# A float32 encoder layer on one core: the x tiles load first, and the Strassen operand T2 of both FFNs is formed tile by tile

## The chip, the cores and the metric

The kernel runs on one core of one Trainium2 chip. The metric is the device time of one execution in microseconds (us); the median of three runs before the change is 1804.01 us (1801.94 to 1806.21). A core has five engines that work through their own instruction lists in order: TensorE (PE, matmuls and transposes), VectorE (DVE), ScalarE (ACT), GpSimd (POOL) and SyncE (SP, which here only issues DMAs). They wait for one another through semaphores.

## The reference

One layer on x of 1024 tokens by 1024 channels, all float32:

```python
x = x + 0.5 * swiglu(rmsnorm(x, ffn1_norm), ffn1_w_gate, ffn1_w_up, ffn1_w_down)   # hidden 2816
h = rmsnorm(x, mix_norm) @ w_in             # -> u, v, c_q, c_kv, k_rope
y_a = gmlp_mixer(u, v, ...)                 # gated MLP over blocks of 128 tokens
y_b = mla_mixer(c_q, c_kv, k_rope, ...)     # 8 heads, block-causal attention
x = x + concat(rmsnorm(y_a), rmsnorm(y_b)) @ w_out
x = x + 0.5 * swiglu(rmsnorm(x, ffn2_norm), ffn2_w_gate, ffn2_w_up, ffn2_w_down)
x = rmsnorm(x, final_norm)
```

with `swiglu(h, g, u, d) = (silu(h @ g) * (h @ u)) @ d`.

## The kernel before

**Numbers.** A float32 operand is split into a high and a low part (`h` and `l`); every product is three 128x512 matmuls, high by high, high by low and low by high. The split is one ACT cast (the high part) and one DVE subtraction (the low part).

**Gate and up.** `GateUp` ("a" is FFN1, "b" is FFN2) computes the gate and up projections in the seven-product scheme of Strassen. The transposed, normalised x is cut into four blocks: B11 and B21 are the two channel halves of tokens 0 to 511 (tiles 0 to 3, 128 tokens each), B12 and B22 those of tokens 512 to 1023 (tiles 4 to 7). The x operands are B11, B21, B22 and the sums T3 = B22 - B12, T2 = T3 + B11, T1 = B12 - B11, T4 = B21 - T2. The weight columns are worked through in 11 units u of 256 gate and 256 up columns; each unit has the products P1 (B11), P2 (B21), P6 (T2), P5 (T1), P7 (T3), P3 (B22) and P4 (T4), 24 matmuls each. `GU_ORDER` begins with P1 and P2 of u0 and of u1 (`EARLY`), which need tiles 0 to 3 only, and then takes P6, P5, P7, P3, P4 of u0, the same of u1, and so on. So the 96 matmuls of `EARLY` stand between the arrival of tiles 0 to 3 and the first use of T2.

**The x operands.** `XOps.tile(i)` normalises one tile (a Square with a sum on ACT, a mean on DVE, the reciprocal root on POOL, `xn` on DVE), transposes it in eight PE transposes and copies it into two blocks on ACT. After tile 3 it splits B11 and B21. `XOps.sums()`, called in the second step of FFN1 and FFN2 after tile 7, forms all sums and splits from whole blocks, in halves of 128x1024: about 20 DVE operations and 10 ACT casts.

**Where tiles come from.** In FFN1 they are loads of x (`xa0` to `xa7`) in one SP queue with the weights (`raw`, four DMAs of 512 KB per unit). A unit's weights are loaded nine steps ahead (`LEAD_LOAD`), its sums three and its splits two steps ahead. In FFN2 tile t comes out of `out_tile(t)`: 48 matmuls of the out-projection (`wo`), an addition of the residual, which is loaded from `x1d` (`x2_t`), a store to `x2d`, and then `xo2.tile(t)`.

**What sets the order.** The code is a list of `Step`s. A tile framework then reorders the instructions of each engine by its own estimate and assigns buffers and semaphores, so that the instruction order differs from the order of the code. SP issues its DMAs in order, and a DMA whose buffer is not free holds all that follow it.

## Time and profile before

| | |
|---|---|
| median of 3 runs | 1804.01 us (1801.94 to 1806.21) |
| the profiled execution | 1804.58 us |
| its span | 1802.8 us |
| PE busy | 1731.7 us, 96% |
| DVE busy | 1122.5 us, 62% |
| ACT busy | 750.3 us, 42% |
| POOL busy | 124.9 us, 7% |

A busy time is the sum over the instructions of an engine. [...] A timeline row gives the start, the duration, the engine, the line, the operation with output and input, and in brackets the idle time of the engine just before and who ended it.

### The profile page before, as it was taken

To read this page: it belongs to the slowest core of one execution; us is meant where nothing else is said; L and a number is where in the kernel's file an instruction comes from. 1 tells how busy PE (TensorE), PEld (TensorE's weight loads), DVE (VectorE), ACT (ScalarE), POOL (GpSimd) and SP (SyncE) were. 2 spreads that over 40 slices of the span, in tenths; PEclk is the share of its full clock that TensorE was granted. 3 is DMA by queue.
4 is the path that set the end of the run, shared out by engine and by line. 5 is a ranking of instruction groups with operands and counts; after the bars stand their busy time and mean duration, and the time that the engine had idled before them with its cause. 6 is when DMAs were issued, how large, how long until landed. Compare 5 with 4: busy or idle time off the path is not lost.

```text
span 1802.8 us, 21101 instructions
## 1 busy us (share of the span) xinstructions
PE 1731.7 (96%) x8196; PEld 1444.9 (80%) x8196; DVE 1122.5 (62%) x1481; ACT 750.3 (42%) x1139; POOL 124.9 (7%) x242
## 2 busy tenths in 40 slices
PE   6799999999999999997999999889999999999988
PEld 5688888888888888896888888668888888888876
DVE  6875466654687667458676544665556655658753
ACT  6533233334343353355666733433233333433442
POOL 2000000000000004225000500000000000000000
PEclk9899999999999999998999899989999999999999
DMA  6132423225834520300000452131323222783431
GB/s 204 59 117 88 135 93 117 88 94 210 292 129 158 192 88 20 109 13 1 1 1 7 142 174 71 53 118 58 134 101 111 88 95 87 245 308 102 158 121 47
DMA packets 123493, 199.51 MB, mean 111 GB/s; under 512 B 11008, under 2 KB 57600, under 8 KB 123392
## 3 DMA queue, kind: packets, MB, share of 16 engines
q1 hardware_dynamic: 122816, 197.11, 32.0%
q8 instruction: 64, 1.05, 0.2%
q10 hardware_dynamic: 576, 1.05, 0.2%
q14 instruction: 37, 0.30, 0.1%
HBM read 143.07 MB, written 55.05 MB: 110 GB/s over the span
## 4 chain that ended last, share of the span: by engine, by line
PE 91%; DVE 4%; ACT 2%; DMA 1%; SPq 1%; issue 1%; POOL 1%; POOLq 0%; ACTq 0%; DVEq 0%
PE psum L438 45%; PE psum L569 8%; PE psum L570 8%; PE psum L567 7%; PE psum L693 2%; PE psum L691 2%; PE psum L692 2%; PE psum L1093 2%; PE psum L1091 2%; PE psum L1090 2%; PE psum L993 2%; PE psum L963 1%; PE psum L286 1%; PE psum L1002 1%; PE psum L1003 1%; PE psum L965 1%
## 5 line engine op out<-in xcount | busy, mean ns | idle before, releaser
L454 DVE TENSOR_TENSOR P_b<-psum,P_b 128x1024 f32<-128x1024 f32 x33 | 40.3, 1222 | 62.8 <-PE psum L438 62.7
L454 DVE TENSOR_TENSOR P_a<-psum,P_a 128x1024 f32<-128x1024 f32 x33 | 40.3, 1221 | 55.6 <-PE psum L438 55.5
L968 DVE TENSOR_REDUCE nm<-psum 128x1 f32<-128x128 f32 (+3 forms) x64 | 47.8, 753 | 27.9 <-PE psum L966 19.8
L444 ACT COPY P_a<-psum 128x1024 f32<-128x1024 f32 x33 | 33.5, 1014 | 68.6 <-PE psum L438 68.6
L444 ACT COPY P_b<-psum 128x1024 f32<-128x1024 f32 x33 | 33.5, 1014 | 68.1 <-PE psum L438 68.1
L455 ACT ACTIVATE P_a<-P_a 128x512 f32<-128x512 f32 x33 | 20.9, 634 | 96.8 <-DVE P_a L454 96.5
L455 ACT ACTIVATE P_b<-P_b 128x512 f32<-128x512 f32 x33 | 20.9, 633 | 96.4 <-DVE P_b L454 96.3
L277 DVE TENSOR_TENSOR pl<-psum,ph 128x384 fp32r<-128x384 f32 (+1 forms) x80 | 48.8, 629 | 11.6 <-ACT ph L276 11.3
L970 ACT ACTIVATE p<-psum,nm 128x128 f32<-128x128 f32 (+3 forms) x64 | 47.9, 749 | 18.9 <-DVE nm L968 17.1
L963 PE MATMUL psum<-kh,qh 96*128 96x512 f32 (+2 forms) x96 | 41.4, 431 | 11.8 <-ACT qh L951 8.1
L257 POOL TENSOR_TENSOR r_fin<-ms_fin,mhalf 128x1 f32<-128x1 f32 x8 | 6.0, 754 | 643.6 <-DVE ms_fin L255 643.6
L1090 PE MATMUL psum<-woh,yh 128*128 128x512 f32 x128 | 50.5, 397 | 0.0
L1091 PE MATMUL psum<-wol,yh 128*128 128x512 f32 x128 | 50.1, 393 | 0.0
L276 ACT CAST ph<-psum 128x384 fp32r<-128x384 f32 (+1 forms) x80 | 41.6, 550 | 9.0 <-PE psum L993 7.9
L438 PE MATMUL psum<-xT2h_f,S2h_b 128*128 128x512 f32 x88 | 35.4, 402 | 10.1 <-ACT S2h_b L423 10.1
L993 PE MATMUL psum<-ident,p 128*128 128x128 f32 x288 | 43.5, 280 | 1.4 <-ACT p L970 1.2
L1002 PE MATMUL psum<-ph,vv 128*128 128x256 f32 x160 | 44.7, 305 | 0.1
L1003 PE MATMUL psum<-pl,vv 128*128 128x256 f32 x160 | 43.5, 301 | 0.3 <-DVE pl L277 0.3
L257 POOL TENSOR_TENSOR r_m<-ms_m,mhalf 128x1 f32<-128x1 f32 x8 | 5.6, 704 | 551.3 <-DVE ms_m L255 551.3
L1093 PE MATMUL psum<-woh,yl 128*128 128x512 f32 x128 | 43.5, 395 | 0.0
L438 PE MATMUL psum<-xT2l_f,S2h_a 128*128 128x512 f32 x88 | 35.1, 399 | 8.3 <-DVE xT2l_f L361 8.3
L438 PE MATMUL psum<-xT1l_f,S1h_b 128*128 128x512 f32 x88 | 34.7, 396 | 6.0 <-DVE xT1l_f L361 6.0
(519 smaller groups left out, 5717.8 us busy)
## 6 DMA issues: line engine op xcount, KB each, us to landing
raw_a<-in_ffn_w_gate SPq DMA_DIRECT2D x22, 512.0 KB, 4.2
...
```

What stands on the lines that cost most here:

```text
L438: mm(o, lhs[:, 4 * m + k, :], rhs[:, k, :], start=pn in FIRST and n == 0, stop=n == 11, skip_group_check=True)
L444: nc.scalar.copy(ev[u, pn], bk)
L454: nc.vector.tensor_tensor(c, bk, c, op=ALU.add)
L567: mm(banks[t], hh[:, j, tl], dh[:, j, :], start=pn in DOWN_FIRST and c == 0 and j == 0, stop=False, skip_group_check=True)
L569: mm(banks[t], hh[:, j, tl], dl[:, j, :], start=False, stop=False, skip_group_check=True)
L570: mm(banks[t], hl[:, j, tl], dh[:, j, :], start=False, stop=c == 5, skip_group_check=True)
L993: nc.tensor.transpose(ps[:, i * P:(i + 1) * P], prs[j][:, c * P:(c + 1) * P], ident)
L1002: mm(acc[:, 0:256], mx["vv"][c][:, h, :], hi, start=i == 0, stop=False)
L1003: mm(acc[:, 0:256], mx["vv"][c][:, h, :], lo, start=False, stop=i == len(pts) - 1)
L1090: mm(pe[e], yh[:, k, :], wh[:, es], start=k == 0, stop=False)
L1091: mm(pe[e], yh[:, k, :], wl[:, es], start=False, stop=False)
L1093: mm(pe[e], yl[:, k, :], wh[:, e * 512:(e + 1) * 512], start=False, stop=k == KD - 1)
```

## The change

It does four things. First, in FFN1 the loads of `xa1`, `xa2` and `xa3` stand in a row ahead of the first unit's weights. Second, `XOps.tile` calls `second(i)` for the tiles 4 to 7, which forms T3, T2 with its split, and B21 - T2 for the 128 columns of that tile: four DVE operations and one ACT cast of 128x512 elements each. Third, `sums` is gone; T1, T3, B22 and T4 are made by `rest`, in the steps +2, +3, +3 and +4 of the FFN, and tied behind the last T2 operations by an issue order (`after`). Fourth, the weights of FFN2's first two units are loaded in the steps of out tile 6 and of P1(u0) rather than nine steps ahead of their products.

```diff
             if i == 3:
                 self.split("B11", self.b[0, 0])
                 self.split("B21", self.b[1, 0])
+            if i >= 4:
+                self.second(i, slice(c, c + P))
+
+        def second(self, i, cs):
+
+            b11, b12, b21, b22 = (v[:, :, cs] for v in (self.b[0, 0], self.b[0, 1], self.b[1, 0], self.b[1, 1]))
+            if i == 4:
+                self.t3 = tile_([P, 4, 512], f"t3_{self.nm}")
+                self.ops["T2"] = [tile_([P, 4, 512], f"xT2{n}_{self.nm}", F32R) for n in "hl"]
+            t3, hi, lo = (v[:, :, cs] for v in (self.t3, *self.ops["T2"]))
+            t2 = tile_([P, 4, P], f"t2{i}_{self.nm}")
+            nc.vector.tensor_tensor(t3, b22, b12, op=ALU.subtract)
+            nc.vector.tensor_tensor(t2, t3, b11, op=ALU.add)
+            self.last = (nc.scalar.copy(hi, t2), nc.vector.tensor_tensor(lo, t2, f(hi), op=ALU.subtract))
+            nc.vector.tensor_tensor(b21, b21, t2, op=ALU.subtract)
...
-        def sums(self):
-            b11, b12, b21, b22 = self.b[0, 0], self.b[0, 1], self.b[1, 0], self.b[1, 1]
-            t3 = tile_([P, 4, 512], f"t3_{self.nm}")
-            t2 = tile_([P, 4, 512], f"t2_{self.nm}")
-            for a, b in HALVES:
-                nc.vector.tensor_tensor(t3[:, a:b], b22[:, a:b], b12[:, a:b], op=ALU.subtract)
-                nc.vector.tensor_tensor(t2[:, a:b], t3[:, a:b], b11[:, a:b], op=ALU.add)
-                nc.vector.tensor_tensor(b21[:, a:b], b21[:, a:b], t2[:, a:b], op=ALU.subtract)
-                self.split("T2", t2, ((a, b),))
...
+        def rest(self, key):
+            with nc.after(*self.last):
+                self.rest_of(key)
...
                         if (u, k) not in loaded:
-                            st.before(LEAD_LOAD - k, lambda u=u, k=k: self.load(u, k))
+                            lead = st.index - load_at[u] if u < len(load_at) else LEAD_LOAD - k
+                            st.before(lead, lambda u=u, k=k: self.load(u, k))
...
-    xts.append(row_tile(x[rows(1), :], "xa1"))
-    gu1.load(0, 0)
-    xts += [row_tile(x[rows(t), :], f"xa{t}") for t in (2, 3)]
-    gu1.load(0, 1)
+    xts += [row_tile(x[rows(t), :], f"xa{t}") for t in (1, 2, 3)]
+    for k in range(2):
+        gu1.load(0, k)
...
-    steps[2].do(xo1.sums)
+
+    def rest(xo, at):
+        for key, j in (("T1", 2), ("T3", 3), ("B22", 3), ("T4", 4)):
+            steps[at + j].do(lambda key=key: xo.rest(key))
+
+    rest(xo1, 0)
...
-    gu2.steps(GU_ORDER)
-    steps[base2 + 1].do(xo2.sums)
+    gu2.steps(GU_ORDER, load_at=(base2 - 2, base2))
+    rest(xo2, base2)
```

Since the framework orders each engine anew, the change is seen in the order of instructions. DVE at the start of FFN1, before the change, from `xn` of tile 7 on (`t_f` is T3 or T2, `P_a` and `hA_a` belong to the products):

```order
L291 SCALAR_TENSOR_TENSOR xn_f_401<-xa_133,r_f_406,g_101 128x1024
L456 TENSOR_TENSOR hA_a_375<-P_a_289 128x512
L368 TENSOR_TENSOR t_f_462<-b_f_314,b_f_310 128x1024 x2
L369 TENSOR_TENSOR t_f_465<-t_f_462,b_f_153 128x1024
L373 TENSOR_TENSOR b_f_310<-b_f_310,b_f_153 128x1024
L361 TENSOR_TENSOR xB22l_f_500<-b_f_314,xB22h_f_499 128x1024 x2
L369 TENSOR_TENSOR t_f_465<-t_f_462,b_f_153 128x1024
L373 TENSOR_TENSOR b_f_310<-b_f_310,b_f_153 128x1024
L361 TENSOR_TENSOR xT3l_f_492<-t_f_462,xT3h_f_491 128x1024
L370 TENSOR_TENSOR b_f_156<-b_f_156,t_f_465 128x1024
L454 TENSOR_TENSOR P_a_458<-psum,P_a_458 128x1024
L361 TENSOR_TENSOR xT3l_f_492<-t_f_462,xT3h_f_491 128x1024
```

The first half of `xT2l` is the next row there. The same engine and place now, from the T3 and T2 pieces of tile 7 to `xT1l`:

```order
L376 TENSOR_TENSOR t_f_316<-b_f_313,b_f_309 128x4x128
L378 TENSOR_TENSOR xT2l_f_320<-t_f_420,xT2h_f_319 128x4x128
L377 TENSOR_TENSOR t_f_446<-t_f_316,b_f_155 128x512
L379 TENSOR_TENSOR b_f_158<-b_f_158,t_f_446 128x4x128
L378 TENSOR_TENSOR xT2l_f_320<-t_f_446,xT2h_f_319 128x4x128
L397 TENSOR_TENSOR b_f_309<-b_f_309,b_f_155 128x1024 x2
L477 TENSOR_TENSOR P_a_491<-psum,P_a_491 128x1024
L387 TENSOR_TENSOR xT3l_f_546<-t_f_316,xT3h_f_544 128x1024 x2
L447 TENSOR_TENSOR S1l_a_508<-S_a_363,S1h_a_505 128x1024
L387 TENSOR_TENSOR xT1l_f_498<-b_f_309,xT1h_f_496 128x1024 x2
```

`xT2l` stood behind eight operations on B22, T3 and T1 and is now ahead of all of them; the pieces of the tiles 4 to 6 stand further up, from `xn` of tile 6 on, and between `xn` of tile 7 and the last `xT2l` there are 17 operations.

SP around the out tiles 5 to 7, before the change (`x_5`, `x_6`, `x_7` are the residual rows, `x2d` the stores; the weights of u0 and u1 of FFN2 were issued further up):

```order
L297 DMA x_4_10679<-x1d 128x1024
L297 DMA y_10757<-yAd 128x512
L1097 DMA x2d<-x_4_10679 128x1024
L297 DMA x_5_10785<-x1d 128x1024
L1097 DMA x2d<-x_5_10785 128x1024
L297 DMA x_6_10865<-x1d 128x1024
L1097 DMA x2d<-x_6_10865 128x1024
L297 DMA x_7_10944<-x1d 128x1024
L1097 DMA x2d<-x_7_10944 128x1024
```

and now, with the semaphores that each waits for (the DVE count of `x_5` is that of the `xT2l` piece of tile 4):

```order
L1125 DMA x2d<-x_4_10686 128x1024 [waits DMAHW4_49,DVE_49]
L308 DMA raw_b_10885<-in_ffn_w_gate 128x4x256 [waits DVE_49,Activation_49]
L308 DMA raw_b_10885<-in_ffn_w_up 128x4x256 [waits DMAHW3_49]
L308 DMA x_6_10901<-x1d 128x1024 [waits PE_49]
L308 DMA raw_b_10889<-in_ffn_w_gate 128x4x256 [waits DMAHW1_49,DMAHW0_49,PE_49]
L308 DMA raw_b_10889<-in_ffn_w_up 128x4x256
L308 DMA x_5_10805<-x1d 128x1024 [waits DMAHW7_49,DVE_49]
L1125 DMA x2d<-x_5_10805 128x1024 [waits DMAHW7_49,DVE_49]
L308 DMA x_7_10987<-x1d 128x1024 [waits PE_49]
```

The four weight loads of u0 stand among the residual loads, and `x_5` is loaded behind `x_6` and behind the T2 piece of tile 4, whose buffer it takes. On DVE, in the same place:

```order
L378 TENSOR_TENSOR xT2l_f_10768<-t_f_10770,xT2h_f_10767 128x4x128
L1124 TENSOR_TENSOR x_5_10805<-psum,x_5_10805 128x512 x2
L266 TENSOR_SCALAR ms_f_10862<-ss_f_10860 128x1
L1124 TENSOR_TENSOR x_6_10901<-psum,x_6_10901 128x512
L302 SCALAR_TENSOR_TENSOR xn_f_10859<-x_5_10805,r_f_10864,g_10314 128x1024
```

`xn` of tile 5 (`xn_f_10859`) now follows the T2 piece of tile 4 and the first addition of tile 6; PE transposes it between the matmuls of out tile 6 and those of out tile 7.

ACT at the start of attention, before the change (`r_qk` is the root for the q and k norms of one tile, `qh` and `kh` the scaled q and k of a head, `p` the exponentials):

```order
L951 ACTIVATE kh_7532<-psum,gkcol 96x512
L883 COPY kn_7481<-psum 128x8x64
L886 ACTIVATE sk_7491<-kn_7481 128x512
L263 ACTIVATE r_qk_7438<-ssq_7418 128x16
L263 ACTIVATE r_qk_7504<-ssq_7485 128x16
L951 ACTIVATE qh_7528<-psum,gqcol 96x512
L970 ACT_TABLE_LOAD
L970 ACTIVATE p_0_7577,rs_0_7568<-psum,nm_0_7573 128x128
```

and now:

```order
L979 ACTIVATE qh_7548<-psum,gqcol 96x512
L979 ACTIVATE kh_7553<-psum,gkcol 96x512
L911 COPY kn_7501<-psum 128x8x64
L914 ACTIVATE sk_7511<-kn_7501 128x512
L274 ACTIVATE r_qk_7458<-ssq_7440 128x16
L998 ACT_TABLE_LOAD
L998 ACTIVATE p_0_7599,rs_0_7591<-psum,nm_0_7596 128x128
L998 ACTIVATE p_1_7609,rs_0_7591<-psum,nm_1_7605 128x256
L998 ACTIVATE p_2_7620,rs_1_7611<-psum,nm_2_7616 128x384
L287 CAST ph_0_1_7632<-psum 128x384
L274 ACT_TABLE_LOAD
L274 ACTIVATE r_qk_7524<-ssq_7505 128x16
```

The `qh` of the first heads moved ahead of both `r_qk`, and the `r_qk` of tile 7 moved behind three exponentials, with a table load before and one after it.

## Rows read from the trace of the kernel before

**Rows 1.** Page, part 1: busy us, share of the span, instructions of each engine.

```profile
PE 1731.7 (96%) x8196; PEld 1444.9 (80%) x8196; DVE 1122.5 (62%) x1481; ACT 750.3 (42%) x1139; POOL 124.9 (7%) x242
```

**Rows 2.** Waits of PE, 0 to 100 us: us in total, times, longest.

```profile
PE psum L438 <- DVE xT2l_f L361: 8.3, 1, 8.3
```

**Rows 3.** Waits of PE, 1120 to 1190 us, the start of FFN2.

```profile
PE psum L438 <- ACT S2h_b L423: 10.1, 1, 10.1
PE psum L438 <- DVE xT1l_f L361: 6.0, 1, 6.0
```

**Rows 4.** Waits of PE, 820 to 870 us, the start of attention.

```profile
PE psum L963 <- ACT qh L951: 8.1, 1, 8.1
PE psum L963 <- DVE kl L952: 2.9, 1, 2.9
```

**Rows 5.** Timeline of PE at the start of FFN1: start, us, instruction, idle before.

```profile
22.01 0.73 PE L438 MATMUL psum<-xB11h_f,A11h_a 128*128 128x512 f32 x2 [1.62 <-ACT xB11h_f L360]
...
50.83 0.39 PE L438 MATMUL psum<-xB21h_f,A12l_a 128*128 128x512 f32 x1
...
61.13 0.80 PE L438 MATMUL psum<-xT2l_f,S2h_a 128*128 128x512 f32 x1 [8.35 <-DVE xT2l_f L361]
...
64.63 0.39 PE L438 MATMUL psum<-xT2h_f,S2h_a 128*128 128x512 f32 x1
...
91.48 0.39 PE L438 MATMUL psum<-xT2h_f,S2h_a 128*128 128x512 f32 x1
```

**Rows 6.** Windows: width, busy us (count) of PE, PEld, DVE, ACT, POOL; PEclk.

```profile
24.00:26.00 2.00, 2.00 (x5) 1.63 (x6) 2.00 (x3) 2.00 (x3) 0.00 (x0) 0.50 1.11 350
68.00:70.00 2.00, 1.80 (x8) 1.17 (x8) 2.00 (x3) 1.31 (x2) 0.00 (x0) 1.00 0.00 0
842.00:844.00 2.00, 0.00 (x0) 0.00 (x0) 2.00 (x4) 1.41 (x3) 1.89 (x4) 0.69 0.00 0
```

**Rows 7.** Timelines of ACT and POOL at the start of FFN1.

```profile
7.99 1.06 ACT L272 ACTIVATE xn_f<-xa 128x1024 f32<-128x1024 f32 x1 [2.17 <-DMA xa<-in_x]
...
16.57 1.05 ACT L423 CAST A12h_a<-raw_a 128x1024 fp32r<-128x1024 f32 x1 [0.92 <-DMA raw_a<-in_ffn_w_up]
...
31.23 2.22 POOL L647 COPY gkcol<-graw 64x1 f32<-64x1 f32 x1
...
33.42 0.56 POOL L257 TENSOR_TENSOR r_f<-ms_f,mhalf 128x1 f32<-128x1 f32 x1
```

**Rows 8.** Timeline of DVE at the start of FFN1.

```profile
46.23 2.36 DVE L368 TENSOR_TENSOR t_f<-b_f,b_f 128x1024 f32<-128x1024 f32 x2 [3.99 <-ACT b_f L350]
...
59.85 1.22 DVE L361 TENSOR_TENSOR xT2l_f<-t_f,xT2h_f 128x1024 fp32r<-128x1024 f32 x1
```

**Rows 9.** Timeline of PE from the end of the out tiles into FFN2.

```profile
1142.76 0.39 PE L438 MATMUL psum<-xB11h_f,A11h_b 128*128 128x512 f32 x1
...
1152.96 1.03 PE L286 MATMUL psum<-ident,xn_f 128*128 128x128 f32 x8
...
1179.95 0.79 PE L438 MATMUL psum<-xT2h_f,S2h_b 128*128 128x512 f32 x1 [10.07 <-ACT S2h_b L423]
...
1184.49 0.39 PE L438 MATMUL psum<-xT2h_f,S2h_b 128*128 128x512 f32 x1
```

**Rows 10.** Timeline of DVE, the first sums of FFN2.

```profile
1154.88 2.36 DVE L368 TENSOR_TENSOR t_f<-b_f,b_f 128x1024 f32<-128x1024 f32 x2 [1.49 <-ACT b_f L350]
```

**Rows 11.** Timelines of SP (the load's issue) and DVE, out tile 6.

```profile
1126.62 0.32 SPq L297 DMA_DIRECT2D x<-x1d  x1
...
1130.27 1.29 DVE L1096 TENSOR_TENSOR x<-psum,x 128x512 f32<-128x512 f32 x2 [7.82 <-DMA x<-x1d]
...
1133.66 1.28 DVE L291 SCALAR_TENSOR_TENSOR xn_f<-x,r_f,g 128x1024 f32<-128x1024 f32 x1 [0.73 <-POOL r_f L257]
```

**Rows 12.** Timeline of ACT at the start of attention.

```profile
851.26 0.22 ACT L263 ACTIVATE r_qk<-ssq 128x16 f32<-128x16 f32 x1 [6.06 <-DVE ssq L892]
...
854.45 1.28 ACT L970 ACT_TABLE_LOAD   x1
```

More of the change, by code (lines that the diff above doesn't have):

```diff
@@ L1 @@
-from contextlib import ExitStack
+from contextlib import ExitStack, nullcontext
 from fractions import Fraction
@@ L117, in identity, with after @@
         pass
+    def after(self, *instructions):
+        return nullcontext()
 GRAIN = 128
@@ L166, in __init__ @@
         self.at = {"sb": place(dry.bufs["sb"], floats // GRAIN, GRAIN), "ps": place(dry.bufs["ps"], 8, 1)}
+        self.tc = tc
         self.sizes = {k: [b[0] for b in v] for k, v in dry.bufs.items()}
@@ L208, in identity, with after @@
         make_identity(self.nc, ap)
+    def after(self, *instructions):
+        stack = ExitStack()
+        for i in instructions:
+            stack.enter_context(self.tc.issue_after(i.ins))
+        return stack
 FLOATS = 51 * 1024 - 512
@@ L361, in split, with rest_of @@
                 nc.vector.tensor_tensor(lo[:, a:b], src[:, a:b], f(hi[:, a:b]), op=ALU.subtract)
-        def sums(self):
-            b11, b12, b21, b22 = self.b[0, 0], self.b[0, 1], self.b[1, 0], self.b[1, 1]
-            t3 = tile_([P, 4, 512], f"t3_{self.nm}")
-            t2 = tile_([P, 4, 512], f"t2_{self.nm}")
-            for a, b in HALVES:
-                nc.vector.tensor_tensor(t3[:, a:b], b22[:, a:b], b12[:, a:b], op=ALU.subtract)
-                nc.vector.tensor_tensor(t2[:, a:b], t3[:, a:b], b11[:, a:b], op=ALU.add)
-                nc.vector.tensor_tensor(b21[:, a:b], b21[:, a:b], t2[:, a:b], op=ALU.subtract)
-                self.split("T2", t2, ((a, b),))
-            for a, b in HALVES:
-                nc.vector.tensor_tensor(b12[:, a:b], b12[:, a:b], b11[:, a:b], op=ALU.subtract)
-                self.split("T1", b12, ((a, b),))
-            self.split("T3", t3)
-            self.split("B22", b22)
-            self.split("T4", b21)
+        def rest(self, key):
+            with nc.after(*self.last):
+                self.rest_of(key)
+        def rest_of(self, key):
+            b11, b12 = self.b[0, 0], self.b[0, 1]
+            if key == "T1":
+                for a, b in HALVES:
+                    nc.vector.tensor_tensor(b12[:, a:b], b12[:, a:b], b11[:, a:b], op=ALU.subtract)
+                    self.split("T1", b12, ((a, b),))
+            else:
+                self.split(key, {"T3": self.t3, "B22": self.b[1, 1], "T4": self.b[1, 0]}[key])
     PRODUCTS = (("P1", "A11", "B11", "a"), ("P2", "A12", "B21", "b"), ("P6", "S2", "T2", "a"), ("P5", "S1", "T1", "c"),
@@ L469, in hsum, with steps @@
             nc.vector.tensor_tensor(t, self.h[u, x0], self.h[u, x1], op=op)
-        def steps(self, order, floor=0, loaded=()):
+        def steps(self, order, floor=0, loaded=(), load_at=()):
             at = {}
```

## The prediction

> **What bounds the kernel now.** I read the page's busy times first, then the waits of PE over the whole span, then the timelines where PE waits. PE is busy 1731.7 of 1802.8 us [rows 1], so the matmuls set the time and only the 71 us in which PE stands still, and the matmuls it does at a low clock, can be won by moving work. The waits that the edited lines cause are at two places. At the start of FFN1 PE waits 8.3 us for `xT2l` [rows 2]; at the start of FFN2 6.0 us for `xT1l` and 10.1 us for `S2h_b`, which stands on ACT behind work that waits for DVE's sums [rows 3]. A third place, the start of attention, has 2.9 and 8.1 us [rows 4]; the change has no line there, but the new order touches it. Elsewhere PE runs its 128x512 matmuls at 0.227 us, as the 24 of a product do.
>
> At FFN1 the timeline gives the whole loss. The first product begins at 22.01 us, P2 of u1 ends at 50.83 + 0.23 = 51.06, T2 begins in earnest at 61.13, and the last product of u0 ends at 91.48 [rows 5]. Between 51.06 and 91.48 stand 120 matmuls, 120 x 0.227 = 27.2 us, so 13.2 us are lost. Part is clock: from 61.13 to 64.63 eight matmuls take 3.50 us where 1.81 would do [rows 5], 1.7 us lost. The clock had fallen also after the shorter waits before 24 us and at 842 us, but at 68 to 70 us, with 0.2 us idle, it stayed at 1.00 [rows 6].
>
> **Part 1: x tiles first.** Tile 1's load is used at 7.99 us and the last weight load of u0 at 16.57, six loads later [rows 7]: 1.43 us per load. Tiles 2 and 3 pass two weight loads, so they land 2.9 us earlier. ACT, which does the Squares, the copies and the weight casts, takes some of it back; I take 2.3 us and the first product at 19.7. The weights move back by as much, P1's from 7.99 + 2 x 1.43 = 10.9 to 13.7, P2's stay at 16.6, both before 19.7: no cost. From there PE has 96 matmuls (21.8), four times eight transposes (3.5, each time under the 1.03 of [rows 9]), a fall of the clock (1.7) and some 1.6 of waits for B11 and B21, as the 1.62 ahead of 22.01 [rows 5]: P2 of u1 ends at 48.3, if the transposes of tiles 6 and 7 are not late. They are in time, but barely: POOL's root for tile 5 is begun only at 33.42 us, behind `gkcol` and its like, which wait for a late load of `graw` [rows 7]. Tiles 4 and 5 now get ahead of these, and tile 6 takes that place: `xn` of tile 6 at 33.42 + 0.56 + 1.28 = 35.3, that of tile 7, behind a weight sum and a T3 piece, at 35.4 + 1.2 + 0.65 + 1.28 = 38.5. PE wants them at 35.5 (P1 to 28.3, 24 matmuls and two times eight transposes) and 38.6 (ten matmuls and eight transposes more).
>
> **Part 2: T2 by tiles.** Before, DVE starts the sums at 46.23 and reaches the first half of `xT2l` at 59.85, without a gap [rows 8]; the order shows eight operations of 128x1024 ahead of it that T2 doesn't need. Now the pieces run from the arrival of tile 4 on. A pair of 128x512 operations takes 1.29 us [rows 11], a 128x1024 in a row 2.36 / 2 = 1.18 [rows 8]: sixteen pieces cost 8 x (1.29 - 1.18) = 0.9 us more than eight wholes. From the end of `xn` of tile 7 (38.5) to the last `xT2l` stand 14 pieces, two wholes and one 128x512: 15 x 0.65 + 2 x 1.18 = 12.1, so T2 is complete at 50.6, and PE, free at 48.3, waits 2.3 us instead of 10.0. The piece of tile 7 also needs its transposes, at about 43: it is DVE's list, not PE, that ends last.
>
> [...]
>
> **Part 3: the other sums behind it.** T1 now follows: two sums, `P_a`, two `xT3l`, `S1l`, the first `xT1l`, 7 x 1.14 = 8.0 after 50.6, so 58.6. PE ends T2 at 50.6 + 5.4 = 56.0 and waits 2.6 us for T1. Then 96 matmuls (T1, T3, B22, T4) without a stall, since T3 is split before T1: 58.6 + 21.8 = 80.4 against 91.48, a gain of 11.1. A fall of the clock in one of the two waits (1.7 us, partly absorbed by the second wait) takes 0.6 on average: **10.5 us**. Bounds: both waits at a low clock and tile 6 two us late, 5.7; no fall and T1 half covered, 12.5.
>
> **Part 4: FFN2.** Before, 15 matmuls of P1 stand among those of the last out tile, which ends at 1142.76; tile 7 is transposed at 1152.96; after those 0.9 us stand 36 matmuls and a pair of T1, to 1152.96 + 0.9 + 38 x 0.227 = 1162.5, then the two waits, and the clock is back at 1184.49 [rows 9]. From 1162.5 to 1184.5 pass 22.0 us for 13 matmuls (2.9): **19.1 us lost**. Now the out tiles end 15 x 0.227 = 3.4 earlier at 1139.36, and 60 matmuls bring the transposes to the same 1152.96. Before, DVE began 1.92 us after that [rows 10]; four pieces and a cast make T2 ready at about 1157.4, while 36 more matmuls keep PE until 1162.0: covered by 4.6 us. `xT1l` comes seven DVE operations later, at 1166, PE wants it at 1167.4: covered, by 1.4 only. All 19.1 us go.
>
> A new wait comes. `x_5` is now loaded behind the T2 piece of tile 4. Backwards from 1139.36, out tile 7 (48 matmuls, 8 transposes) starts at 1127.6 and out tile 6 (12 transposes) at 1114.6, so tile 4 is transposed from 1115.5; 1.9 on, a `yl`, four pieces and a cast put the piece's end at 1121.1; a residual load takes 1130.27 - 1126.62 = 3.65, and from the addition to the end of `xn` pass 1133.66 + 1.28 - 1130.27 = 4.7 [rows 11]. So `xn` of tile 5 is ready at 1129.5, and PE wants it between out tiles 6 and 7, at 1126.7: 2.8 us, and half a fall of the clock, 0.9: **3.7 us**. The weights of u0 and u1, now issued from about 1112 to 1133 (an estimate from the out tiles that they wait for), take 8 x 1.43 us and are wanted at 1139 and 1150: hidden, and if not, the third rival. Net gain 15.4; bounds 19.1 (no new wait) and 10 (2.8 + 1.7, and 4.6 for T1 or the weights).
>
> **Part 5: attention, by reordering.** ACT's `r_qk` waits 6.06 us for DVE at 851.26 with the first `qh` behind it; a table load takes 1.28 [rows 12]. The `qh` now go first, but two more table loads stand between the exponentials: 6.06 - 2 x 1.28 = **3.5 us**. The trace doesn't show the new order, so bounds: 8.1 [rows 4] and -2.6, the loads alone. Down and the other stages keep their work; I book nothing.
>
> **The sum.** 10.5 + 15.4 + 3.5 = 29.4 from the profiled execution's 1804.6, which is 0.6 above the median: 1775.2, less that, about **1775 us**. Low end 1804.6 - (12.5 + 19.1 + 8.1) = 1765; high end 1804.6 - (5.7 + 10 - 2.6) = 1791.
>
> **Rivals.** First, DVE and POOL keep what the order gives: if the roots of tiles 6 and 7 come 2 us later on POOL, every DVE operation behind `xn` of tile 7 follows, and in FFN2 T1 loses its cover of 1.4. For it: POOL's late root, DVE without a gap from 46 to 60 us [rows 8], covers of 0.1 us. Against it: tiles 4 and 5 are out of the way. FFN1 would gain 6, FFN2 12, attention nothing: 1787.
>
> Second, the clock: the long waits become three short ones (2.3, 2.6, 2.8), and if each ends at a low clock, as the 2.9 us wait did [rows 4, 6], that is 3 x 1.7 = 5.1 where 1.5 is booked: 1779. [...]
>
> Third, slower: SP's queue. Weights and residual rows now share it in the out tiles, and `x_5` holds all behind it until DVE has done a T2 piece. If `x_5`, `x_6` and `x_7` were each exposed with the whole chain (3.65 + 4.7), two weight loads ahead (2.9) and a fall of the clock (1.7), that is 3 x 12.9 = 39 us, 35 more than booked: 1810. It decides from 33 us, 11 for each of three tiles. Against it: `x_6` and `x_7` wait only for out tiles that end one tile before they are wanted, 11.8 us.
>
> Fourth, more gain: no new wait at `x_5` and attention freed of its 8.1: 1766.
>
> Fifth, nothing: the framework's new order loses in stages that I haven't costed (29 us, in many small waits) what it gains here: 1804. The order shows the intended moves, so it must be lost elsewhere.
>
> **How the numbers follow.** Forecast (1769 to 1783) 0.54, clock 0.12, DVE and POOL 0.16, more gain 0.08, nothing 0.05, slower 0.05. The range 1765 to 1791 takes in the first four with their bounds. About 0.2% (3.6 us) is what a measurement of this kernel can tell from no change: faster 0.90, same 0.05, slower 0.05.
>
> **What would show it.** PE's waits in the first 100 us: two of 2 to 3 us, for `xT2l` and `xT1l`, and none of 8; T2 of u1 at about 80 to 82 us instead of 91.5. Between the out tiles and T4 of FFN2 no wait over 1 us, and one of about 3 us for `xn` between out tiles 6 and 7. `qh` ahead of `r_qk` in attention and 3 us less idle PE there. I am wrong if PE waits longer for tile 6 or 7 in FFN1 than for T2, if T1 stalls FFN2, or if the stages in between take over 5 us more.

## The result, and the profile after

| | before | after |
|---|---|---|
| median, same chip | 1803.18 us (1801.94 to 1806.21, 4 runs) | 1780.54 us (1777.81 to 1782.51, 4 runs) |
| the profiled execution | 1804.58 us | 1778.92 us |
| its span | 1802.8 us | 1777.1 us |

The ratio is 0.9871, 95% interval 0.985 to 0.9891: 22.6 us less by the medians, 25.7 us less between the two profiled executions. The forecast was 1775 us in a range of 1765 to 1791. The sign and the range held, and the time came out 5.5 us above the forecast; the parts of the sum did much worse than their total, as the stages show.

Part 1 of the page of after: busy us, share of the span, instructions of each engine.

```profile
PE 1732.5 (97%) x8196; PEld 1445.7 (81%) x8196; DVE 1122.3 (63%) x1497; ACT 750.5 (42%) x1145; POOL 127.4 (7%) x242
```

Against [rows 1] PE does the same work in the same busy time; what fell is the time in which it stands still, 71.1 us before and 44.6 now (span less busy). That balance holds for the whole span only: in attention, below, less idle time went with more busy time.

**FFN1.** Waits of PE in after, 0 to 100 us: who is waited for, us in total, times, longest (the two longest of the products' matmuls; the transposes wait for the first tiles, as before). In after a product's matmul is L461, a split L386 (ACT) and L387 (DVE); line numbers shift from kernel to kernel.

```profile
PE psum L461 <- ACT xB11h_f L386: 2.6, 1, 2.6
PE psum L461 <- DVE xT1l_f L387: 1.9, 1, 1.9
```

Timeline of PE in after, the rows that answer [rows 5]: the first product, the start of T2 of u0, the wait for T1, the start of T2 of u1.

```profile
19.25 1.22 PE L461 MATMUL psum<-xB11h_f,A11h_a 128*128 128x512 f32 x2 [2.62 <-ACT xB11h_f L386]
...
48.42 0.61 PE L461 MATMUL psum<-xT2h_f,S2h_a 128*128 128x512 f32 x2
...
56.35 0.50 PE L461 MATMUL psum<-xT1l_f,S1h_a 128*128 128x512 f32 x1 [1.88 <-DVE xT1l_f L387]
...
77.79 0.39 PE L461 MATMUL psum<-xT2h_f,S2h_a 128*128 128x512 f32 x1
```

The wait of 8.3 us for `xT2l` [rows 2] is gone altogether: T2 begins at 48.42 with no bracket behind it. T2 of u1 begins at 77.79 instead of 91.48, 13.7 us earlier. A window of after over that stretch shows that the clock didn't fall at the 1.9 us wait (width, busy us and count of PE, PEld, DVE, ACT, POOL, then PEclk, the granted clock of PE as a share of its full speed):

```profile
40.00:80.00 40.00, 38.12 (x170) 31.27 (x169) 39.42 (x45) 23.13 (x28) 0.00 (x0) 1.00 0.27 92
```

**FFN2.** Waits of PE in after, 1080 to 1190 us, all that there are, and the two DVE rows behind the first (out tile 5: the residual's addition, then `xn`).

```profile
PE psum L297 <- DVE xn_f L302: 2.7, 1, 2.7
PE psum L1118 <- ACT b_f L361: 0.3, 1, 0.3
```

```profile
1109.51 1.29 DVE L1124 TENSOR_TENSOR x<-psum,x 128x512 f32<-128x512 f32 x2 [4.29 <-DMA x<-x1d]
...
1112.94 1.28 DVE L302 SCALAR_TENSOR_TENSOR xn_f<-x,r_f,g 128x1024 f32<-128x1024 f32 x1
```

Both stalls of [rows 3], 10.1 and 6.0 us, are gone, and the one new wait of any size is that for `xn` of tile 5, whose residual row `x_5` comes late: its load is issued at 1105.24 and DVE can use it at 1109.51.

**Attention.** Waits of PE in after, 820 to 870 us, the three longest.

```profile
PE psum L991 <- ACT p L998: 2.1, 1, 2.1
PE psum L991 <- ACT kh L979: 2.0, 1, 2.0
PE psum L1021 <- DVE kl L980: 1.5, 1, 1.5
```

The 8.1 us for `qh` of [rows 4] are broken up into waits of at most 2.1. The stage is none the shorter for it: 214.1 us from the last matmul of the K and V projections to the last matmuls of attention's output fold, against 214.2 before. Windows of PE over the stage, before and then after (width, busy us and count of PE, PEclk, DMA share, GB/s):

```profile
838.94:1053.14 214.20, 198.53 (x1286) 0.93 0.14 44
825.25:1039.33 214.08, 202.70 (x1293) 0.94 0.12 38
```

PE's idle time fell by 4.3 us, from 15.7 to 11.4, and its busy time rose by 4.2 for nearly the same work (1286 and 1293 matmuls). The run e10 below shows where that busy time comes from.

**Down.** Timelines of PE and ACT in after at product P7 of FFN2's second Down half ("b"): the wait, and the cast that ended it.

```profile
1722.65 0.80 PE L591 MATMUL psum<-wT3h_b,aS3h_b 128*128 128x512 f32 x1 [7.37 <-ACT aS3h_b L564]
```

```profile
1721.56 1.04 ACT L564 CAST aS3h_b<-aS_b 128x1024 fp32r<-128x1024 f32 x1 [4.47 <-DMA out<-o]
```

ACT waits there for the store of an output tile: the place in SBUF of `aS3h_b` is that of `o`, the normalised final row, until `o` has gone out (e7 below tests this). PE's clock was 1.00 from 1710 to 1715 us, ahead of the wait, and 0.50 behind it; window of PE in after, the 6 us behind the wait:

```profile
1722.65:1728.65 6.00, 6.00 (x14) 0.50 0.00 0
```

Before, PE waited at the same product for `wT3l_b`, a split that stood in DVE's list behind the final norms; there a store of `o` held another split of this product, and only for 0.42 us. Waits of PE in before, 1720 us to the end, and that row of DVE:

```profile
PE psum L569 <- DVE wT3l_b L550: 5.3, 1, 5.3
```

```profile
1745.22 1.23 DVE L541 TENSOR_TENSOR aS3l_b<-aS_b,aS3h_b 128x1024 fp32r<-128x1024 f32 x1 [0.42 <-DMA out<-o]
```

Put together by stages, from the PE milestones of the two profiled executions:

| stretch | forecast gain | measured |
|---|---|---|
| to T2 of u1 in FFN1 | 10.5 | 13.7 |
| from there to the end of attention's fold | 3.5 | 0.1 |
| out-projection and FFN2 to T2 of its u1 | 15.4 | 15.8 |
| rest of FFN2's gate and up, Down | 0 | -0.6 |
| P7 of Down b | 0 | -3.3 |
| sum | 29.4 | 25.7 |

### The profile page after: what moved, and what is told of

Same layout as the page of the kernel before. It is cut to its first block, busy times and chain, and to the rows that moved or that the text cites. A ratio compares the mean times of both kernels' runs of the same rounds, so it can differ in the third digit from the quotient of the medians.

```text
span 1777.1 us, 21155 instructions
## 1 busy us (share of the span) xinstructions
PE 1732.5 (97%) x8196; PEld 1445.7 (81%) x8196; DVE 1122.3 (63%) x1497; ACT 750.5 (42%) x1145; POOL 127.4 (7%) x242
## 5 line engine op out<-in xcount | busy, mean ns | idle before, releaser
L288 DVE TENSOR_TENSOR pl<-psum,ph 128x384 fp32r<-128x384 f32 (+1 forms) x80 | 48.7, 628 | 12.5 <-ACT ph L287 11.7
L998 ACT ACTIVATE p<-psum,nm 128x384 f32<-128x384 f32 (+4 forms) x64 | 47.7, 747 | 16.7 <-DVE nm L996 16.4
L991 PE MATMUL psum<-kh,qh 96*128 96x512 f32 (+2 forms) x96 | 40.5, 425 | 6.2 <-ACT p L998 2.7
L605 DVE SCALAR_TENSOR_TENSOR x_b<-psum,x_b 128x512 f32<-128x512 f32 x32 | 21.2, 686 | 36.9 <-PE psum L594 36.9
L461 PE MATMUL psum<-xB11h_f,A11h_a 128*128 128x512 f32 x88 | 35.5, 406 | 2.6 <-ACT xB11h_f L386 2.6
L1021 PEld LDWEIGHTS psum<-ident,p 128*128 128x128 f32 x288 | 33.5, 144 | 4.9 <-DVE kl L980 1.8
```

The costliest lines, as they stand in the source:

```text
L288: nc.vector.tensor_tensor(lo, src, f(hi), op=ALU.subtract)
L461: mm(o, lhs[:, 4 * m + k, :], rhs[:, k, :], start=pn in FIRST and n == 0, stop=n == 11, skip_group_check=True)
L998: nc.scalar.activation(pr[:, 0:n], ps[:, 0:n], AF.Exp, bias=nm, accum_out=mx["sum", h, t // 2][:, t % 2:t % 2 + 1])
L1021: nc.tensor.transpose(ps[:, i * P:(i + 1) * P], prs[j][:, c * P:(c + 1) * P], ident)
```

## The experiments

The theory: each half of the change acts by itself and where the prediction put it; the attention stage and Down's P7 are not touched by any edited line and moved because the placing of buffers and the clock came out differently. The rivals: that the T2 wait would have gone by the load order alone; that whole 128x1024 operations as early as the pieces would do as well; that attention's lost gain is ACT's table loads.

All stage lengths, in us, from the trace of each kernel's profiled execution: "FFN1" from the first P1 to T2 of u1, "attention" from the last K/V projection matmul to the last fold matmul, "FFN2" from there to T2 of u1, "P7" from Down b's P7 to its P4. The last two columns are timed runs: the median of this kernel, and its ratio to before on the same chip with the 95% interval.

| kernel | FFN1 | attention | FFN2 | P7 | median | ratio |
|---|---|---|---|---|---|---|
| before | 69.5 | 214.2 | 156.5 | 37.2 | 1803.18 | 1 |
| after | 58.5 | 214.1 | 140.8 | 40.5 | 1780.54 | 0.9871 [0.985, 0.9891] |
| e1_x_first | 71.3 | 215.4 | 159.1 | 40.2 | 1804.08 | 1.001 [1.0, 1.0021] |
| e2_ffn1_only | 58.5 | 208.3 | 155.7 | 37.7 | 1786.09 | 0.991 [0.9894, 0.9927] |
| e3_ffn2_only | 70.3 | 212.4 | 141.2 | 38.9 | 1791.32 | 0.9949 [0.9934, 0.9963] |
| e5_whole_t2 | 62.3 | 204.8 | 145.5 | 34.5 | 1772.83 | 0.9837 [0.9823, 0.9852] |
| e6_reach | 61.9 | 211.8 | 147.1 | 32.0 | 1774.48 | 0.9832 [0.981, 0.9854] |
| e7_in_place | 58.6 | 214.0 | 144.2 | 29.9 | 1767.72 | 0.9804 [0.9784, 0.9824] |
| e8_x5_early | 58.6 | 208.2 | 136.8 | 39.8 | 1772.79 | 0.9823 [0.9802, 0.9845] |
| e9_rqk_pool | 58.6 | 213.9 | 143.2 | 40.5 | 1783.19 | 0.9887 [0.9865, 0.9908] |
| e10_both | 58.5 | 216.5 | 136.8 | 29.9 | 1765.24 | 0.9789 [0.9774, 0.9803] |
| e11_whole_in_place | 62.5 | 204.3 | 146.0 | 29.9 | 1769.81 | 0.9818 [0.9803, 0.9832] |
| e12_before_reach | 69.6 | 202.7 | 159.1 | 34.4 | 1794.04 | 0.9952 [0.9938, 0.9967] |
| e13_both_reach | 61.8 | 210.3 | 141.2 | 29.9 | 1766.20 | 0.9798 [0.9781, 0.9814] |

**e1_x_first: the load order alone, in the kernel before.**

```diff
-    xts.append(row_tile(x[rows(1), :], "xa1"))
-    gu1.load(0, 0)
-    xts += [row_tile(x[rows(t), :], f"xa{t}") for t in (2, 3)]
-    gu1.load(0, 1)
+    xts += [row_tile(x[rows(t), :], f"xa{t}") for t in (1, 2, 3)]
+    for k in range(2):
+        gu1.load(0, k)
```

> The kernel before with the load order alone changed (x tiles 1 to 3 ahead of the first weights). Theory (DVE's list after tile 7 sets the start of T2, the loads only the start of P1): the first product starts about 2.8 us earlier, 19.2 instead of 22.0, but T2 of u1 comes at most 3 us earlier than 91.5, 88.5 to 91, and the time is 1800 to 1803. Rival (the earlier tiles carry the gain of FFN1): T2 of u1 at 78 to 83 and 1790 to 1795.

Measured 1804.08 us (1801.23 to 1810.81), no difference from before and 1 us over the expected range. Waits of PE in e1_x_first, 0 to 100 us:

```profile
PE psum L438 <- DVE xT2l_f L361: 8.4, 1, 8.4
```

The first product starts 2.4 us earlier, at 19.60, and T2 of u1 only 0.6 earlier, at 90.92: the 8.4 us for `xT2l` are the 8.3 of [rows 2] over again. Earlier tiles are worth nothing while DVE's whole sums stand in front of T2.

**e2_ffn1_only and e3_ffn2_only: each half alone.** e2 keeps the pieces and the load order for FFN1 and gives FFN2 the old `sums` and the old weight loads; e3 does the reverse.

```diff
-    xo2 = XOps("f2")
+    xo2 = XOps("f2", tiled=False)
...
-    gu2.steps(GU_ORDER, load_at=(base2 - 2, base2))
-    rest(xo2, base2)
+    gu2.steps(GU_ORDER)
+    steps[base2 + 1].do(xo2.sums)
```

```diff
-    xo1 = XOps("f1")
+    xo1 = XOps("f1", tiled=False)
...
-    rest(xo1, 0)
+    steps[2].do(xo1.sums)
```

> The change in FFN1 alone: loads, pieces and the sums behind them; FFN2 as before. Theory (the gains add, 13.7 in FFN1 and 15.4 in FFN2): T2 of u1 at 77.8 as with the whole change, the two waits of 6 and 10 us at FFN2 as before, 1788 to 1791. If attention (8.1 and 2.9 us before) and the end of Down b move though no line of theirs differs from either kernel, that is the buffer placement. Rival (FFN1's gain is lost again before the end, at attention): the start of attention is not 13 us earlier, and 1797 or more.

> The change in FFN2 alone: pieces, the sums behind them, the late weight loads; FFN1 as before. Theory: T2 of u1 in FFN1 at 91.5 as before; no wait over 1 us between the out tiles and T4 of FFN2, one of about 2.7 us for xn of tile 5 between out tiles 6 and 7; FFN2 gains 15 us and the time is 1786 to 1790, give or take 4 for Down b. Rival (the gain in FFN2 needs FFN1's change, by the order or the placement): less than 8 us gained.

Measured 1786.09 us (1785.69 to 1786.55) for e2 and 1791.32 us (1790.01 to 1801.01) for e3. Waits of PE at the start of FFN2, in e2 and in e3, 1080 to 1205 us:

```profile
PE psum L477 <- ACT S2h_b L462: 10.1, 1, 10.1
PE psum L477 <- DVE xT1l_f L387: 6.0, 1, 6.0
```

```profile
PE psum L297 <- DVE xn_f L302: 3.1, 1, 3.1
```

Each half does its part and nothing of the other's. e2 reaches T2 of FFN1's u1 at 77.66 us, after at 77.79, and keeps the two stalls of [rows 3] to the tenth; e3 brings FFN2 to 141.2, after 140.8, and brings the wait for `x_5`; its time lies 1.3 us over what was expected. The ratios add up as well: 0.9% and 0.51% make 1.41%, after has 1.29% with an interval of 1.09 to 1.5. e2 came out 2 us faster than expected; its attention stage took 208.3 us rather than 214, and no line of attention differs.

**e5_whole_t2: T2 as early, but in wholes.** The sums behind tile 7 in two halves of 128x1024, T2 first, everything else as in after. It tells whether forming T2 tile by tile matters, or only that it goes first.

```diff
-            if i >= 4:
-                self.second(i, slice(c, c + P))
+            if i == 7:
+                self.second()
...
+            for a, b in HALVES:
+                s = slice(a, b)
+                nc.vector.tensor_tensor(self.t3[:, s], b22[:, s], b12[:, s], op=ALU.subtract)
+                nc.vector.tensor_tensor(t2[:, s], self.t3[:, s], b11[:, s], op=ALU.add)
+                self.last = (nc.scalar.copy(hi[:, s], t2[:, s]),
+                             nc.vector.tensor_tensor(lo[:, s], t2[:, s], f(hi[:, s]), op=ALU.subtract))
+                nc.vector.tensor_tensor(b21[:, s], b21[:, s], t2[:, s], op=ALU.subtract)
```

> The changed kernel, but T2 is formed after tile 7 from whole blocks, in halves of 128x1024, still ahead of T1, T3, B22 and T4. Theory (the pieces matter): in FFN1 T2's eight operations start at about 44 and end at 53, T1 follows 8 us later at 61, so PE waits 3 to 5 us for T2 and again 2 to 3 for T1, and T2 of u1 comes 4 to 6 us later than 77.8; in FFN2 T2 is late by 1 to 3 us; the time is 1784 to 1789. Rival (the order is all: it is enough that T2 is ahead of the other sums): waits as with the change, within 2 us of it, 1779 to 1783.

Measured 1772.83 us (1771.98 to 1773.85): faster than the change. Read by the total, the pieces would be a loss of 8 us. Read by stages it is the other way round. Waits of PE in e5, 0 to 100 us, and at the start of FFN2:

```profile
PE psum L461 <- DVE xT1l_f L387: 3.3, 1, 3.3
...
PE psum L461 <- DVE xT3l_f L387: 0.5, 1, 0.5
PE psum L461 <- DVE xT2l_f L378: 0.3, 1, 0.3
```

```profile
PE psum L461 <- DVE xT1l_f L387: 3.7, 1, 3.7
PE psum L461 <- DVE P_b L477: 1.1, 1, 1.1
```

The two stages that the pieces are about are longer without them, FFN1 by 3.8 us (62.3 against 58.5) and FFN2 by 4.8 (145.5 against 140.8): the wait moves from T2 to T1. What e5 wins, 9.3 us in attention and 6.0 in P7, lies in stages whose code is the same. So the pieces do gain, 3.8 and 4.8 us; the rest of the change's 13.7 and 15.8 comes without them, with T2 ahead of the other sums. In FFN2 the 4.8 us are what is left after the wait for `x_5`, which the pieces bring and which e5 doesn't have: against e8 below, which has the pieces without that wait (136.8), e5 is 8.7 longer. The load order and the late weight loads stay in e5; what T2 first would be worth without them wasn't tested. That T2 itself hardly waits here (0.3 us) was not expected; I had looked for a longer one, and for a time of 1784 or more.

**e6_reach and e12_before_reach: another placing of the buffers.** A routine gives every buffer its place in SBUF so that two users of one place lie far apart in the program, as far as `REACH` matmuls; past that any place is as good. Changing the constant changes no computation, only who waits for whose buffer, and with it the order that the framework chooses. e6 is after with it, e12 before with it.

```diff
-REACH = 160.0
+REACH = 150.0
```

> The changed kernel with one constant of the buffer placement changed (REACH 160 to 150); no instruction is added, removed or moved in the code. Theory (attention's start and the end of Down b move with the placement, not with the change's own edits): FFN1 (T2 of u1 at 77.8) and FFN2's start stay within 2 us, attention and Down b move by 2 to 5 us against the changed kernel, either way, and the time by up to 6. Rival (those stages follow from the change itself): all stages within 0.5 us, the time within 2.

> The kernel before with one constant of the buffer placement changed (REACH 160 to 150), no other edit. Theory (the placement alone moves the kernel before as it moves the changed one, which lost 6 us): between 1795 and 1810, with FFN1 and FFN2 within 3 us and attention and Down b moved by 2 to 8. Rival (the kernel before is settled in its stages): within 2 us of 1803.

Measured 1774.48 us (1771.8 to 1776.58) for e6, 6.1 less than after, and 1794.04 us (1792.1 to 1795.05) for e12, 8.5 us less than before, without any of the change. Waits of PE in e12, at the start of attention (820 to 870 us) and of FFN2:

```profile
PE psum L963 <- ACT kh L951: 2.0, 1, 2.0
PE psum L947 <- ACT p L970: 1.1, 2, 0.7
```

```profile
PE psum L438 <- ACT S2h_b L423: 16.2, 1, 16.2
```

The 8.1 us for `qh` are gone from attention (202.7 us instead of 214.2), although neither the loads nor the sums were edited, and the two stalls of FFN2 fall together into one of 16.2. In e6 the placing helps P7 (32.0) and harms the change's own stages, by 3.4 us in FFN1 and 6.3 in FFN2, where at most 2 were expected: DVE does weight sums between the pieces, and T2 waits again. e12's attention moved by 11.5, more than the 8 expected, and its time lies 1 us under the expected range. Waits of PE in e6, 0 to 100 us:

```profile
PE psum L461 <- DVE xT1l_f L387: 1.7, 1, 1.7
...
PE psum L461 <- DVE xT2l_f L378: 1.1, 1, 1.1
...
PE psum L461 <- ACT xT2h_f L378: 0.8, 1, 0.8
```

What follows: one placing constant moved these two totals by 6.1 and 8.5 us, in a case of two versions 22.6 apart. A sum over edited stages can't forecast that, and a total can't judge one edit; the stages, read with their waits, say more, though the placing moves them too.

**e7_in_place: the final row written in place.** If P7's wait is the store of `o`, normalising tiles 0 to 3 into the residual tile takes it away: `o` then only holds what ACT's Square writes, and the store leaves from `x3`.

```diff
-        normed(x3, mx["gf"], o, f"fin{t}")
-        nc.sync.dma_start(out[rows(t), :], o)
+        normed(x3, mx["gf"], o, f"fin{t}", out=x3)
+        nc.sync.dma_start(out[rows(t), :], x3)
```

> The changed kernel with the final norm of tiles 0 to 3 written in place, so that the stores leave from x and the buffer that aS3h of P7 waits for is free once ACT's Square is done. Theory (the 7.4 us wait in P7 of Down b is a buffer held by the stores of out): the wait falls below 2 us, with it the low clock behind it, and the time is 7 to 9 us under the changed kernel, 1771 to 1774. Rival (the wait comes from DVE and ACT being behind with the splits): another split is late at the same place, 4 us or more of wait remain, and the time is within 3 us of the changed kernel.

Measured 1767.72 us (1766.58 to 1771.93), 12.8 less than after, where 7 to 9 were expected. Window of e7_in_place that holds its P7:

```profile
1702.00:1733.00 31.00, 31.00 (x139) 25.66 (x138) 24.97 (x32) 15.52 (x24) 3.91 (x4) 1.00 0.35 125
```

PE is busy through all 31 us at a clock of 1.00, and P7 takes 29.9 us instead of 40.5. The 10.6 us are the 7.4 of the wait and 3.2 behind it, where after's clock was 0.50 for 6 us. All four kernels with this edit have 29.9; the others lie between 32.0 and 40.5.

The profiled execution of e7 shows one thing more. PE and POOL have after's order from first to last, and DVE and ACT up to the final norms, yet FFN2 takes 144.2 us instead of 140.8. Waits of PE in e7_in_place, 1080 to 1205 us, the longest:

```profile
PE psum L297 <- DVE xn_f L302: 4.6, 1, 4.6
```

The load of `x_5` took 6.1 us from issue to landing here and 4.2 in after. So the wait for `x_5` isn't a fixed 2.7 us; it is 3.1 in e3, 3.8 in e9 and 4.1 in e6.

**e8_x5_early: `x_5` one out tile sooner.** If the 2.7 us wait is the late issue of one residual row, moving that load alone removes it.

```diff
-        x2 = row_tile(x1d[rows(t), :], f"x2_{t}")
+        x2 = mx["x2", t]
...
+    for t in range(NT):
+        ws_[t].before(1 if t == 5 else 0, lambda t=t: x_load(t), ws_[0].index)
```

> The changed kernel with the residual row of tile 5 loaded one out tile earlier, ahead of the weights and not behind the T2 piece of tile 4. Theory (the 2.7 us wait for xn of tile 5 comes from that load): the wait is gone, and the stretch from the out tiles to T2 of FFN2 is 2.5 to 4 us shorter; elsewhere only what the placement moves. Rival (DVE is late with xn anyway, the T2 pieces stand ahead of it): 2 us or more of wait for an xn remain in the out tiles.

Measured 1772.79 us (1768.11 to 1774.47). There is no wait of PE at all from 1080 to 1205 us, and FFN2 takes 136.8 us, 4.0 less. The other 3.7 by the medians lies outside the edited stage: attention took 208.2 us in the profiled execution, with the code untouched. Other ways to free the queue (all weight loads or all residual rows earlier) were not tried.

**e9_rqk_pool: attention without the two table loads.** If the loads eat the gain of the shorter `qh` wait, taking `r_qk`'s root to POOL brings it back.

```diff
-        rr = rsqrt_table(ssq, f"qk{t}", 16)
+        rr = small(f"r_qk{t}", 16)
+        nc.gpsimd.tensor_tensor(rr, ssq, mhalf, op=ALU.pow)
```

> The changed kernel with the roots of the q and k norms (r_qk) made on POOL by a power instead of on ACT by a square root with a correction on DVE; so the two extra table loads among the first exponentials are gone, and five DVE and ACT operations per tile. Theory (the two table loads, 2.6 us, and ACT's wait for r_qk take back what the earlier qh gains): the idle time of PE at the start of attention falls from 7.2 to 4 us or less and the stage is 3 to 6 us shorter. Rival (DVE's work on q and k of tiles 6 and 7 and the low clock bound the stage): idle time moves to other waits, and the stage is within 1.5 us of the changed kernel.

Measured 1783.19 us (1780.8 to 1786.77), attention 213.9 us, as in after. Waits of PE in e9, 820 to 870 us:

```profile
PE psum L976 <- ACT kn L911: 8.0, 1, 8.0
```

Without the table loads one long wait is back, 8.0 us for another operand of ACT, and the stage is as long; the theory's 3 to 6 us didn't come. As the order changed with the edit, e9 alone doesn't clear the table loads. e8 does: up to 987 us its engines have after's order, both loads included (ACT has them at 839.82 and 841.35 us), and its stage is 6.0 us shorter than before's.

**e10_both: e7 and e8 together.** Edits as shown.

> The changed kernel with both repairs: the final norm in place (alone 10.6 us less in P7 of Down b) and the residual row of tile 5 loaded early (alone 4 us less from attention's end to FFN2, and 5.9 us less in attention). Theory (the two are at different places and add): P7 of Down b about 30 us long, no wait for xn of tile 5, 1758 to 1766. Rival (the placement moves something else by as much): 1768 or more.

Measured 1765.24 us (1760.65 to 1766.02), ratio 0.9789: the best version, 15.3 us below after. P7 gives 10.6 and `x_5` 4.0, as each did alone. And it shows what moves attention: e8 and e10 have on PE and on POOL the same instructions in the same order from first to last, and on DVE, ACT and SP they differ only in the last norms, more than 600 us behind attention. Yet attention took 208.2 us in e8 and 216.5 in e10. Windows of PE, e8 first, then e10, each 20 to 30 and 30 to 40 us after the last K/V projection matmul (width, busy us and count of PE, PEclk, DMA share, GB/s):

```profile
845.75:855.75 10.00, 8.22 (x50) 0.95 0.01 2
855.75:865.75 10.00, 10.00 (x67) 1.00 0.00 1
```

```profile
845.30:855.30 10.00, 8.02 (x34) 0.67 0.00 0
855.30:865.30 10.00, 10.00 (x37) 0.50 0.01 2
```

The idle time is nearly the same, 1.78 and 1.98 us in the first window. The clock isn't: in e8 it is back at 0.95 there, in e10 PE works a whole window without a gap at 0.50 and does 37 matmuls where e8 does 67. Matched matmul by matmul, e10 loses 7.0 us to e8 between 849 and 866 us of its time, and the other 1.3 behind 985 us. The whole stage, e8 and then e10:

```profile
825.75:1033.96 208.21, 197.92 (x1292) 0.96 0.13 41
825.30:1041.76 216.46, 205.90 (x1292) 0.92 0.12 40
```

Idle time is 10.3 and 10.6 us; the 8.0 us of busy time are the clock's. The two ran on different chips, but one kernel on one chip shows the same: the four executions of e8 took 1768.11, 1771.54, 1774.03 and 1774.47 us at mean granted clocks of 0.990, 0.987, 0.986 and 0.985. The first of them is the profiled one. The 10 us windows for before and after too, 50 us from that matmul on (a matmul that spans two windows counts in both):

| matmuls of PE in | 0-10 | 10-20 | 20-30 | 30-40 | 40-50 | sum | idle us, 0-30 | PEclk, 30-40 |
|---|---|---|---|---|---|---|---|---|
| before | 14 | 14 | 56 | 61 | 73 | 218 | 12.5 | 1.00 |
| after | 26 | 31 | 34 | 55 | 73 | 219 | 7.1 | 0.84 |
| e10_both | 27 | 32 | 34 | 37 | 71 | 201 | 7.1 | 0.50 |
| e8_x5_early | 26 | 31 | 50 | 67 | 75 | 249 | 6.4 | 1.00 |
| e12_before_reach | 25 | 33 | 52 | 68 | 77 | 255 | 5.0 | 1.00 |

After has 5.4 us less idle time than before in the first 30 us and is at the same count at 50: it won the idle time and lost it to a clock that was low while PE worked.

**e11_whole_in_place: wholes or pieces, with P7 out of the way.** e5 and e7 together.

> T2 from whole blocks after tile 7, and the final norm in place: the pair to the run with the pieces and the norm in place. Theory (pieces are worth 4.1 us in FFN1 and about 5 in FFN2; what made the whole T2 faster in all was attention and Down b, by placement): FFN1 and FFN2 again 4 and 3 to 5 us longer than with pieces, Down b alike at 30 to 31; the rest is attention, 9 us less; 1765 to 1770. Rival (whole operations on DVE are better in themselves): FFN1 or FFN2 no longer than with pieces.

Measured 1769.81 us (1768.19 to 1770.19), 2 above e7 and 4.6 above e10. FFN1 is 62.5 us against 58.6, FFN2 146.0 against 144.2: the pieces are worth 3.9 and 1.8 us by stage, and attention, 204.3 here and 214.0 in e7, hides it in the total. The 1.8 is less than the 3 to 5 expected because of e7's 4.6 us for `x_5`; against e10, which has the pieces without that wait, FFN2 is 9.2 longer here.

**e13_both_reach: e10 at the other placing.** Edit as in e6.

> The changed kernel with both repairs, and the placement constant at 150. Theory (repairs of a wait hold under another placement, but attention and single waits move): Down b's P7 stays at 30 to 32 us, and the time is within 6 us of the same kernel at 160. Rival (the repairs were luck of one placement): P7 again over 35 us or a wait of over 2 us for an xn in the out tiles.

Measured 1766.20 us (1765.4 to 1767.4), the same as e10 within the intervals. FFN1 is 3.3 us longer and FFN2 4.4 (a wait of 3.2 for ACT's copy of `P_b`), attention 6.2 shorter, P7 29.9 in both. So P7's repair holds at the other placing; the totals agree because the other stages moved by as much in both directions.

## Why the prediction came out as it did

**Part 1, right.** The first product was put at 19.7 and came at 19.25; P2 of u1 was to end at 48.3, and T2 began at 48.42. e1 shows that the load order yields nothing alone, so its use lies in Part 2.

**Parts 2 and 3, right in mechanism, one term mis-sized.** T2 was to be complete at 50.6 and T1's wait to be 2.6 us; they came at 48.35 and 1.9. (The eight operations that stood ahead of `xT2l` were two each on B22, T3 and T1, one on T4 and one sum of products.) The step that failed is "tile 6 takes that place": I left `gqcol` and `gkcol` at their old 1.68 and 2.22 us [rows 7]. POOL and DVE in after:

```profile
29.49 0.74 POOL L674 TENSOR_SCALAR gqcol<-graw 64x1 f32<-64x1 f32 x1 [1.93 <-DMA graw<-in_q_head_norm]
30.29 1.03 POOL L675 COPY gkcol<-graw 64x1 f32<-64x1 f32 x1
31.28 0.56 POOL L268 TENSOR_TENSOR r_f<-ms_f,mhalf 128x1 f32<-128x1 f32 x1
33.37 1.40 POOL L268 TENSOR_TENSOR r_f<-ms_f,mhalf 128x1 f32<-128x1 f32 x1 [1.53 <-DVE ms_f L266]
```

```profile
30.06 1.22 DVE L447 TENSOR_TENSOR A12l_a<-raw_a,A12h_a 128x1024 fp32r<-128x1024 f32 x1
31.88 1.28 DVE L302 SCALAR_TENSOR_TENSOR xn_f<-xa,r_f,g 128x1024 f32<-128x1024 f32 x1 [0.60 <-POOL r_f L268]
...
34.88 1.27 DVE L302 SCALAR_TENSOR_TENSOR xn_f<-xa,r_f,g 128x1024 f32<-128x1024 f32 x1
...
47.66 0.69 DVE L378 TENSOR_TENSOR xT2l_f<-t_f,xT2h_f 128x512 fp32r<-128x512 f32 x1
```

The two took 0.74 and 1.03 us, 2.13 us less. The root of tile 6 started at 31.28 instead of the 33.42 booked, and `xn` of tile 7 ended at 36.15 where 38.5 was worked out; all the rest of DVE's list moved up with it by about 2.2 us, to a last `xT2l` at 48.35. The 12.1 us that I gave that list came out as 12.2, and that by luck: the sum counts the 17 operations in front of the last `xT2l` and leaves out its own 0.65, and the 128x512 operations follow each other by 0.60 where 0.65 was booked. With no fall of the clock either (0.6 booked), 13.7 us were gained, more than the upper bound of 12.5, which had left POOL as it was.

The pieces cost less than their price. Rows of DVE in after, in a run of 128x512 operations:

```profile
41.35 0.68 DVE L376 TENSOR_TENSOR t_f<-b_f,b_f 128x512 f32<-128x512 f32 x1
41.96 0.68 DVE L379 TENSOR_TENSOR b_f<-b_f,t_f 128x512 f32<-128x512 f32 x1
42.56 0.68 DVE L479 TENSOR_TENSOR hA_a<-P_a 128x512 f32<-128x512 f32 x1
```

Each lasts 0.68 but they start 0.60 or 0.61 apart, and behind a 128x1024 the next operation starts 1.13 or 1.14 after it (37.28, 38.42, 39.55): sixteen pieces are 16 x 0.605 - 8 x 1.135 = 0.6 us dearer than eight wholes, where 0.9 was booked.

**Part 4, right.** The stalls of 19.1 us went; the wait for `xn` of tile 5 was forecast at 2.8 and is 2.70; the net gain was forecast at 15.4 and is 15.8. T1 and the weights were covered, as worked out. e3 shows that this half stands by itself, and e8 that the wait is `x_5`: without it FFN2 gains 4.0 more, where 3.7 was the price. How near the price came is in part luck: with the same order e7 waits 4.6 us, as the load that was priced at 3.65 took 4.2 in after and 6.1 there.

**Part 5, wrong.** 3.5 us were booked and 0.1 came. The step that failed prices the stage by ACT's chain alone (6.06 us less two table loads) and leaves the clock out. The idle time fell by 4.3 us, more than that; but PE's busy time rose by 4.2 for nearly the same work. From 10 to 20 us behind the projections, at a clock of 0.50 in both, PE was idle for 5.5 us in before and for 2.1 in after, and from 30 to 40 us the clock was 1.00 in before and 0.84 in after. e8 shows that the table loads aren't the cause, and e8 against e10 shows the clock by itself at work: 8.3 us between two executions of one order. After, e7, e8 and e10 have the same order on every computing engine up to 987 us, and their stages took 214.1, 214.0, 208.2 and 216.5 us. Against before's 214.2, itself one execution, that order gave 6.0 us in one and cost 2.3 in another; the 0.1 is one draw out of this spread, and what it gives on average stays open.

**"Down and the other stages keep their work; I book nothing", wrong by 3.3 us.** The work was kept, the place of a buffer wasn't: P7 waits 7.4 us for a cast that the store of `o` holds up, where it waited 5.3 before for a split in DVE's list. e7 shows the cause. The trace of before had the place to look at, PE's 5.3 us wait at P7, but not the cause: a store held DVE there for 0.42 us.

**The rivals.** The first (DVE and POOL keep what the order gives) went the other way: POOL was faster. The second (clock) came true at attention, where it wasn't priced. Of the three waits for which it was priced T2's didn't come, at T1's the clock stayed at 1.00, and behind `x_5`'s it was 0.77 (1116 to 1120 us). The third (SP's queue) holds for `x_5` alone, once, and not for `x_6` and `x_7`. The fourth (no wait for `x_5`, and attention freed of its 8.1) didn't come; e8, with an edit of its own, has the first half and 6.0 of the 8.1. The fifth (lost in other stages) is right in kind and covers 3.9 us of 29.

So the 1775 was near by luck, because errors cancelled: +3.2, -3.4, +0.4, -0.6 and -3.3 make -3.7 us; the other 1.8 us to the median are 1.6 by which the profiled execution of after lies under its median, and 0.2 of rounding.
